# Folding the pool groups' maps and scales into the pool projection's weight, in a streaming-encoder block on one Trainium2 core

## The chip, the core and the metric

The kernel runs on one core of a Trainium2 chip. A core has five engines with queues of their own: TensorE (PE in the profile) multiplies matrices and writes PSUM, VectorE (DVE) and ScalarE (ACT) do elementwise work, GpSimd (POOL) and SyncE (SP) are used here mostly to issue transfers. Sixteen DMA engines move data between device memory and the core's SBUF. The metric is the device time of one execution in microseconds, as the median of several runs.

## What is computed

One block of a hybrid encoder on a sequence of 2048 frames with 1024 channels, in float32. The part that matters here is branch A, the pooling branch, and where its result goes:

```python
def pool_mixer(u, pool_w, pool_scale, w_pool_out):
    groups = jnp.split(u, POOL_GROUPS, axis=-1)
    pooled = jnp.stack([trailing_mean_minus_self(g, w) for g, w in zip(groups, POOL_WINDOWS)], axis=2)
    mixed = jnp.einsum('bsgc,gcd->bsgd', pooled, pool_w)
    mixed = mixed.reshape(u.shape) * pool_scale
    return mixed @ w_pool_out
...
    h = rmsnorm(x, norm_mix_pre[l])
    proj = h @ w_in[l]
...
    merged = jax.nn.sigmoid(g_a) * branch_a + jax.nn.sigmoid(g_b) * branch_b
    x = x + rmsnorm(merged @ w_o[l], norm_mix_post[l])
    h = rmsnorm(x, norm_mlp_pre[l])
    f = jnp.square(jax.nn.relu(h @ w_up[l])) @ w_down[l]
    x = x + rmsnorm(f, norm_mlp_post[l])
```

There are four pool groups of 128 channels with windows of 2, 4, 8 and 16 frames. Each group has a 128 x 128 map (`pool_w`) and a scale per channel, then all 512 channels are projected to 1024 (`w_pool_out`). Branch B is a gated convolution of 31 taps with a LayerNorm. Map, scale and projection are linear and follow each other with nothing between, so their product can be formed from the weights alone.

## The kernel before

**Numbers in two parts.** Float32 products are made of three matmuls in TensorE's fp32r format: each operand is split into a high part (ACT casts it to fp32r) and a low part (DVE subtracts the high part), and high x high, high x low and low x high are accumulated (`passes`, `matmuls`). `split` does this for data, `split_w` for weights, which live in the rings `wh` and `wl` of three tiles each; raw weights are loaded into the ring `wr` of four.

**Tiles and stages.** The sequence is cut into two batches b of 1024 tokens, and all tiles are 128 partitions by 1024. Batch 0 runs the input projection first: the GLU octets, then the pool octet, then gates a and b (`run_first`, `run`). An `Octet` is a 2 x 2 block product done in seven products by a Strassen scheme, each of 24 matmuls of 512 columns; after each it calls `flush` (which issues pending stores of kept weights) and `bg()`. Then `branch_a(0)` projects the pooled cells, and the same follows for batch 1, whose weights are partly reloaded from copies kept in device memory (`kept`). Then come `merge(0)`, the output projection of batch 0, `branch_a(1)`, the MLP of batch 0, and the rest of batch 1.

**Background lanes.** Work that is not a main product stands in generators. A `Lane` is given credit at a rate of so many steps per `bg()` call; a generator's plain `yield` ends a step, and `yield n` ends the lane's work for this call and for n - 1 further calls. The lanes carry the statistics of batch 1 (`in_stats`), the convolution (`conv_steps`, 31 taps on DVE per group at L924 and L928, four groups per batch), the pooling (`pool_steps`) and LayerNorm (`norm_steps`). `empty()` runs what is left. In batch 0 the pooling and the convolution's groups 1 to 3 form one chain at rate 3 that starts when the pool octet is done (`more`, L1562); what is left of it goes on in batch 1's lanes at rate 3.2, then 2.8.

**The pool groups.** `pool_steps` (L1012) loads a group's cell u and a window s from device memory, adds shifted windows on DVE, subtracts the cell (L1036), splits the result (L1042), multiplies it with the group's map from `pw` (L1046 to L1049, the tile `mix`), scales it by channel out of PSUM on ACT (L1051) and stores it in `mxd`. `pool_weight` (L1006) loads and splits the maps once.

**The pool projection.** `fetch` (batch 0) or `fetch_spread` (batch 1) loads the four cells of `mxd` and splits them. `branch_a` (L1089) takes four weight tiles of `w_po` with `load_w` (L234): in batch 0 a raw tile is loaded, cast and subtracted, and the low part is stored; in batch 1 the raw tile is loaded and cast, and the low part is loaded. Each weight tile serves 48 matmuls (the tile `A`); gate a is reloaded from `sad`, multiplied in (L1107), and the result goes to `mad`.

**Order.** A planner (the Tile framework's scheduler) orders each engine's instructions by priority, which is the order of tracing moved ahead by an offset: `ahead` is 260 instructions for weights. `behind` places background instructions after the main line's last one. SP's queue holds nearly all transfers and is worked in order, so that a transfer that waits for a tile holds up those behind it. Main products and fold or mix products share one ring of three PSUM tiles (`psum`).

Of the kernel before, what the change touches and what calls it, by code (L numbers as in the profile page):

```python
# [15 lines left out]
P = 128  # L16
D = 1024
# [45 lines left out]
def f32(ap):  # L63
    return ap.bitcast(F32)
# [3 lines left out]
def block_kernel(  # L68
# [35 lines left out]
    def mk(pl, tag, dt=F32, shape=(P, TB)):  # L104
        return pl.tile(list(shape), dt, tag=tag, name=nm(tag))
# [20 lines left out]
    def load(o, src):  # L126
        return nc.sync.dma_start(o, src)  # L127
# [778 lines left out]
    def conv_steps(b, groups, ahead=True):  # L906


        def get(c):
            v = window(TAPS - 1 + TB)  # L910
            load(v, vd[c][:, b * TB : b * TB + TAPS - 1 + TB])
            return v

        v = None
        for c in groups:
            if v is None:
                v = get(c)
                yield 1
            nv = None
            acc = mk(p_y, "y")  # L920
            for k in range(TAPS):
                wk = col(C_CW + c * TAPS + k)
                if k == 0:
                    nc.vector.tensor_scalar(  # L924
                        acc, v[:, :TB], wk, col(C_CB + c), op0=ALU.mult, op1=ALU.add
                    )
                else:
                    nc.vector.scalar_tensor_tensor(  # L928
                        acc, v[:, k : k + TB], wk, acc, op0=ALU.mult, op1=ALU.add
                    )  # L930
                if ahead and k == 15 and c != groups[-1]:
                    nv = get(c + 1)
                yield
            v = nv
            if c == 0:
                sums[b] = mk(p_ss, "sm")
                nc.vector.tensor_copy(sums[b], acc)
            else:
                add(sums[b], sums[b], acc)
            load(yd[b, c, 0], acc)  # L940
            yield
# [61 lines left out]

    pw = [p_const.tile([P, CW], F32R, tag=f"pw{i}", name=f"pw{i}") for i in (0, 1)]

    def pool_weight():  # L1006
        raw = mk(p_wr, "wr")[:, :CW]
        load(raw, w_pool)
        nc.scalar.copy(pw[0], raw)
        sub(pw[1], raw, f32(pw[0]))  # L1010

    def pool_steps(b, alone):  # L1012

# [8 lines left out]
        for g in range(CC):  # L1022
# [15 lines left out]
            )  # L1038
            if g + 1 == CC:
                done.add(("windows", b))  # L1040
            yield 1
            hl = split(u, *TR)  # L1042
            if g + 1 < CC:
                s, u = get(g + 1)
            yield 2
            ps = psum("mix")  # L1046
            for t in (0, 1):
                h = slice(t * T, (t + 1) * T)
                matmuls(ps[:, h], pw, g, [tuple(p[:, h] for p in hl)], main=False)  # L1049
            o = tr()  # L1050
            nc.scalar.activation(o, ps, AF.Copy, scale=col(C_PSC + g))  # L1051
            yield
            load(mxd[b, g, 0], o)
            yield

# [33 lines left out]
    def branch_a(b, mixed, bg):  # L1089
# [7 lines left out]
        keys = [(c, t) for c in range(CPS) for t in (0, 1)]  # L1097
        for (c, t), sg in ahead_by_one(keys, gate_of, 2):
            if t == 0:
                w = load_w(w_po[c], ("po", c))  # L1100
            ps = psum("A")
            for q in (0, 1):
                i = matmuls(ps[:, q * T : (q + 1) * T], w, CC * q, half(mixed, t))
# [456 lines left out]
        lanes.append(tail)  # L1560

    def more():  # L1562
        pool_weight()
        tail.gens.append(chain_of(pool_steps(0, True), conv_steps(0, (1, 2, 3), False)))
        tail.rate = 3

    pi = pool_in(0, parts)[0]
    run_first(o1, then(lambda: lanes.append(stats), then(after_glu, o2, 6)), bg, dve)
    run(
        [then(more, pi)],  # L1570
        gate(0, parts, 3, sad, "ga", "lows"),
        gate(0, parts, 5, sbd, "gb", "sums"),
        left=o2,
    )
    stats.empty()
    rest = tail.gens
    mixed = fetch(mxd, 0)
    parts = Parts(lambda ops: input_parts(1, ops))
# [12 lines left out]
    lanes += [Lane(3.2, *rest, marked(norm_steps(0, 1), "norm"))]  # L1591

    def pooling():
        lanes[0].rate = 2.8
        lanes.append(Lane(1.7, pool_steps(1, False)))
        lanes.append(Lane(1.5, behind_all(conv_steps(1, (0, 1, 2, 3)), "conv", ("windows", 1))))


# [517 lines left out]
```

## Time and profile before

| | us |
|---|---|
| median of three runs | 2207.85 |
| lowest and highest | 2205.48, 2213.11 |
| the profiled execution | 2211.62 |
| its span, from first to last instruction | 2209.8 |
| its mean granted TensorE clock | 0.991 of full speed |

The profile is of one execution. Its rows of time give the busy time of each engine, with the number of instructions behind an x; PEld is the loading of weights into TensorE, which overlaps its matmuls. A row of the timeline has the start, the duration, the engine, the line of the kernel, the operation, out<-in by the program's names, and in brackets the engine's idle time before it with what ended it. L268 is the matmul of the helper `matmuls`, L121 the subtraction helper, L118 the addition helper, L225 the cast of a weight, L127 a load or store on SP's queue. Rows of transfers end with the median time from issue to landing. PEclk is the TensorE clock that was granted, 1.00 being full speed. In a row of tiles three numbers behind a colon are the least, the median and the greatest duration in ns. Rows of groups give busy us, the mean ns of one, and the idle time before them.

In time: gates a and b of batch 0 run to 296 us, the pool projection of batch 0 to 340 us, then the pool octet and the others of batch 1; the pool projection of batch 1 runs from 758 to about 808 us, and the MLP fills the rest.

### The profile page before, as it was taken

What the parts mean: (1) busy time and instruction counts of PE and PEld (TensorE: products, weight loads), DVE (VectorE), ACT (ScalarE), POOL (GpSimd) and SP (SyncE); (2) the same over time, 40 slices, a digit from 0 to 9 for tenths busy, and PEclk for the clock granted to TensorE, in tenths of its full rate; (3) what the DMA queues carried; (4) which work ended last, traced back from release to release, by engine and by line L of the source; (5) the groups of instructions that cost most, each with busy time, mean ns of one, the idle gap of its engine ahead of it and who ended that gap; (6) DMA issues with size and microseconds to landing.
All of it is one profiled execution on the core that took longest, in us unless ns stands there. A gap on an engine that the chain in (4) does not pass through costs nothing. (4 is left out here: it accounts for less than half of the span.)

```text
span 2209.8 us, 25108 instructions
## 1 busy us (share of the span) xinstructions
PE 2167.7 (98%) x9588; PEld 1787.0 (81%) x9588; DVE 1684.4 (76%) x1637; ACT 1050.3 (48%) x1094; POOL 27.0 (1%) x51
## 2 busy tenths in 40 slices
PE   9999999999999999999999999999999999999996
PEld 7888888788888788888888878788778888888875
DVE  8997788998678898977757857776645556696667
ACT  6444454334533545555625766655444222224553
POOL 1000000000000000000000000000000000000001
PEclk9999999999999999999999999999999999999998
DMA  7688897678997687355686768976956545446798
GB/s 274 246 296 320 324 331 275 236 260 294 332 373 248 257 314 276 129 190 201 242 333 226 259 248 294 338 295 232 338 197 229 183 157 189 148 146 221 268 310 254
DMA packets 158264, 568.04 MB, mean 257 GB/s; under 512 B 17696, under 2 KB 17952, under 8 KB 158112
## 3 DMA queue, kind: packets, MB, share of 16 engines
q1 hardware_dynamic: 140608, 503.43, 64.1%
q10 hardware_dynamic: 12672, 46.14, 5.4%
q0 software_dynamic: 4864, 16.87, 2.8%
q8 instruction: 75, 1.23, 0.2%
q14 instruction: 45, 0.37, 0.0%
HBM read 378.58 MB, written 188.84 MB: 257 GB/s over the span
## 5 line engine op out<-in xcount | busy, mean ns | idle before, releaser
L268 PE MATMUL up<-big,wh 128*128 128x512 f32 x1792 | 481.0, 390 | 1.8 <-DVE big L121 1.6
L268 PEld LDWEIGHTS up<-big,wh 128*128 128x128 f32 x1792 | 336.0, 188 | 73.3 <-DVE big L121 2.7
L225 ACT CAST wh<-wr 128x1024 fp32r<-128x1024 f32 x177 | 185.7, 1051 | 313.6 <-PE up L268 72.2
L268 PE MATMUL down<-tr,wh 128*128 128x512 f32 x800 | 312.2, 390 | 0.0
L928 DVE SCALAR_TENSOR_TENSOR y<-v,cst,y 128x1024 f32<-128x1024 f32 x240 | 307.5, 1281 | 2.8
L268 PE MATMUL down<-fo,wh 128*128 128x512 f32 x784 | 303.1, 392 | 1.6 <-ACT fo L1773 1.6
L268 PE MATMUL up<-big,wl 128*128 128x512 f32 x896 | 276.5, 390 | 0.7 <-DVE wl L121 0.7
L268 PE MATMUL down<-fo,wl 128*128 128x512 f32 x768 | 238.4, 392 | 2.7 <-DMA wl<-lows 2.7
L225 ACT CAST wh<-ws 128x1024 fp32r<-128x1024 f32 x118 | 124.0, 1052 | 223.5 <-DVE ws L121 66.6
L268 PEld LDWEIGHTS up<-big,wl 128*128 128x128 f32 x896 | 168.0, 188 | 35.9 <-DVE wl L121 1.2
L118 DVE TENSOR_TENSOR big<-big,down 128x1024 f32<-128x1024 f32 x88 | 106.9, 1219 | 114.6 <-PE down L268 105.9
L1773 ACT CAST fo<-tr 128x1024 fp32r<-128x1024 f32 x86 | 86.8, 1051 | 207.9 <-PE down L268 138.3
L268 PEld LDWEIGHTS down<-tr,wh 128*128 128x128 f32 x800 | 150.7, 188 | 31.4
L268 PEld LDWEIGHTS down<-fo,wh 128*128 128x128 f32 x784 | 147.9, 189 | 33.4 <-ACT fo L1773 2.7
L268 PEld LDWEIGHTS down<-fo,wl 128*128 128x128 f32 x768 | 145.1, 189 | 33.2 <-DMA wl<-lows 3.1
L121 DVE TENSOR_TENSOR wl<-ws,wh 128x1024 fp32r<-128x1024 f32 x110 | 134.2, 1221 | 47.4 <-ACT wh L225 47.3
L121 DVE TENSOR_TENSOR wl<-wr,wh 128x1024 fp32r<-128x1024 f32 x100 | 121.9, 1220 | 31.9 <-ACT wh L225 30.3
L121 DVE TENSOR_TENSOR tr<-tr,fo 128x1024 fp32r<-128x1024 f32 x86 | 101.8, 1220 | 45.5 <-ACT fo L1773 45.5
L268 PE MATMUL wo<-big,wh 128*128 128x512 f32 x480 | 128.9, 390 | 0.0
L268 PE MATMUL glu<-big,wh 128*128 128x512 f32 x464 | 125.4, 391 | 1.2 <-ACT wh L225 0.5
L268 PE MATMUL gb<-big,wh 128*128 128x512 f32 x448 | 120.1, 390 | 0.0
L268 PE MATMUL ga<-big,wh 128*128 128x512 f32 x448 | 120.0, 389 | 0.0
(194 smaller groups left out, 3365.0 us busy)
## 6 DMA issues: line engine op xcount, KB each, us to landing
tr<-fd SPq DMA_DIRECT2D x110, 512.0 KB, 4.6
wl<-kept SPq DMA_DIRECT2D x85, 512.0 KB, 4.7
kept<-wl SPq DMA_DIRECT2D x72, 512.0 KB, 5.9
wr<-w_down SPq DMA_DIRECT2D x68, 512.0 KB, 5.4
wr<-w_up SPq DMA_DIRECT2D x64, 512.0 KB, 4.6
wr<-w_in SPq DMA_DIRECT2D x60, 512.0 KB, 5.3
fd<-tr ACTq DMA_DIRECT2D x54, 512.0 KB, 3.6
fd<-tr SPq DMA_DIRECT2D x48, 512.0 KB, 3.2
```

Source lines behind the costliest of these rows:

```text
L118: return nc.vector.tensor_tensor(o, a, b, op=ALU.add)
L121: return nc.vector.tensor_tensor(o, a, b, op=ALU.subtract)
L225: nc.scalar.copy(hi[:, :n], src[:, :n])
L268: i = nc.tensor.matmul(ps, w[wp][:, (at + k) * P : (at + k + 1) * P], rhs[k][xp], start=start and n == 0, stop=stop and n == len(order) - ...
L928: nc.vector.scalar_tensor_tensor(acc, v[:, k : k + TB], wk, acc, op0=ALU.mult, op1=ALU.add)
L1773: nc.scalar.copy(hi, t)
```

## The change

The maps and scales are now multiplied into the projection's weight once. A new generator `fold_steps` loads the maps (transposed, so that the output channel lies on the partitions), scales them by channel on ACT and splits them into `pw`. For each of the four weight tiles it loads the raw tile, splits it, multiplies it with the four maps (12 matmuls of 256 columns), splits the product, and stores both parts in device memory as `folded`. It has a lane of its own at rate 1 that starts after the second product of gate a's second octet, and is emptied before the projection of batch 0. `folded_weight` replaces `load_w` in `branch_a`: in both batches it loads both parts directly into `wh` and `wl`. `pool_steps` stores the pooled cell itself, without split, product and scaling, and yields less. The convolution's first step of a run of groups now yields 2, not 1, and two lane rates of batch 1 are 3 and 1.5 in place of 2.8 and 1.7. The columns of `w_po` lie in another order in device memory, so that a group's 256 are next to each other; the product is put back in the old order as it leaves PSUM.

```diff
@@ conv_steps
             if v is None:
                 v = get(c)
-                yield 1
+                yield 2
@@
-    def pool_weight():
-        raw = mk(p_wr, "wr")[:, :CW]
-        load(raw, w_pool)
-        nc.scalar.copy(pw[0], raw)
-        sub(pw[1], raw, f32(pw[0]))
+    folded = {(c, p): dram("folded") for c in range(4) for p in (0, 1)}
+
+    def fold_steps():
+        m = mk(p_wr, "wr")[:, :CW]
+        load(m, w_pool)
+        for g in range(CC):
+            gm = m[:, g * P : (g + 1) * P]
+            nc.scalar.activation(gm, gm, AF.Copy, scale=col(C_PSC + g))
+        nc.scalar.copy(pw[0], m)
+        sub(pw[1], m, f32(pw[0]))
+        for c in range(4):
+            raw = tr()
+            load(raw, w_po[c])
+            yield 1
+            hl = split(raw, *TR)
+            yield 2
+            ps = psum("fold")
+            for g in range(CC):
+                h = slice(g * 2 * P, (g + 1) * 2 * P)
+                matmuls(ps[:, h], pw, g, [tuple(x[:, h] for x in hl)], main=False)
+            whole = ps.rearrange("p (g q n) -> p q g n", g=CC, q=2)
+            hi, lo = tr(F32R), tr(F32R)
+            by_q = [x.rearrange("p (q g n) -> p q g n", q=2, g=CC) for x in (hi, f32(hi), lo)]
+            nc.scalar.copy(by_q[0], whole)
+            sub(by_q[2], whole, by_q[1])
+            yield 1
+            load(folded[c, 0], f32(hi))
+            load(folded[c, 1], f32(lo))
+            yield 1
+
+    def folded_weight(c):
+        with tc.high_priority(offset=ahead[0]):
+            w = mk(p_wh, "wh", F32R), mk(p_wl, "wl", F32R)
+            for p in (0, 1):
+                load(f32(w[p]), folded[c, p])
+        return w
@@ pool_steps
-            yield 1
-            hl = split(u, *TR)
+            o = u
             if g + 1 < CC:
                 s, u = get(g + 1)
             yield 2
-            ps = psum("mix")
-            for t in (0, 1):
-                h = slice(t * T, (t + 1) * T)
-                matmuls(ps[:, h], pw, g, [tuple(p[:, h] for p in hl)], main=False)
-            o = tr()
-            nc.scalar.activation(o, ps, AF.Copy, scale=col(C_PSC + g))
-            yield
             load(mxd[b, g, 0], o)
             yield
@@ branch_a
-                w = load_w(w_po[c], ("po", c))
+                w = folded_weight(c)
@@
     def more():
-        pool_weight()
...
+    fold = Lane(1.0, fold_steps())
     pi = pool_in(0, parts)[0]
+    ga = gate(0, parts, 3, sad, "ga", "lows")
+    gb = gate(0, parts, 5, sbd, "gb", "sums")
+    then(lambda: lanes.append(fold), ga[1], 2)
...
     stats.empty()
+    fold.empty()
@@ pooling
-        lanes[0].rate = 2.8
-        lanes.append(Lane(1.7, pool_steps(1, False)))
+        lanes[0].rate = 3
+        lanes.append(Lane(1.5, pool_steps(1, False)))
@@ kernel
-        "w_pool": g["pool_w"].transpose(1, 0, 2).reshape(P, CW),
-        "w_po": pairs(g["w_pool_out"]).reshape(4, P, D),
+        "w_pool": g["pool_w"].transpose(2, 0, 1).reshape(P, CW),
+        "w_po": pairs(g["w_pool_out"]).transpose(0, 1, 3, 2, 4).reshape(4, P, D),
```

More of the change, by code (lines that the diff above doesn't have):

```diff
@@ L1570, in block_kernel @@
         [then(more, pi)],
-        gate(0, parts, 3, sad, "ga", "lows"),
-        gate(0, parts, 5, sbd, "gb", "sums"),
+        ga,
+        gb,
         left=o2,
```

## The prediction

> **What bounds the kernel now.** I read the page first, for the engine that sets the pace; then the busy time by stretch, for where that engine pauses; then its waits, the timeline around the worst pause, and the transfers of the stretch that the change fills.
>
> ```profile
> span 2209.8 us, 25108 instructions
> PE 2167.7 (98%) x9588; PEld 1787.0 (81%) x9588; DVE 1684.4 (76%) x1637; ACT 1050.3 (48%) x1094; POOL 27.0 (1%) x51
> ```
>
> TensorE (PE) is busy for 98% of the span, 42.1 us short of it. A busy PE need not be at its peak, so I look at the spacing of its matmuls:
>
> ```profile
> core 0: us, PE busy (x) PEld busy (x) DVE busy (x) ACT busy (x) POOL busy (x), PEclk, DMA share, GB/s
> 186.00:345.00 159.00, 159.00 (x706) 131.59 (x705) 123.86 (x122) 80.27 (x88) 0.00 (x0) 1.00 0.93 336
> 345.00:400.00 55.00, 50.82 (x211) 40.82 (x210) 50.08 (x43) 20.20 (x20) 0.00 (x0) 0.94 0.62 214
> 396.00:400.00 4.00, 4.00 (x11) 3.11 (x10) 4.00 (x4) 1.05 (x1) 0.00 (x0) 0.50 0.52 148
> 500.00:600.00 100.00, 98.39 (x442) 81.38 (x441) 75.72 (x78) 51.10 (x52) 0.00 (x0) 1.00 0.87 316
> 750.00:815.00 65.00, 62.60 (x276) 51.23 (x275) 60.78 (x64) 30.11 (x37) 4.84 (x9) 0.97 0.84 315
> 1610.00:2085.00 475.00, 475.00 (x2100) 393.37 (x2098) 303.22 (x262) 170.15 (x174) 0.00 (x0) 1.00 0.56 186
> ```
>
> From 1610 to 2085 us 2100 matmuls take 475 us, 226 ns each, at a granted clock of 1.00: there a 512-column matmul costs 226 ns of end time. From 186 to 345 us, where the weight is to be folded, PE has no idle time either. So the kernel is bound by its count of matmuls, plus a few pauses. Two pauses lie where the change reaches: 345 to 400 us (55.00 - 50.82 = 4.2 us) and 750 to 815 us (2.4 us). Each also lowers the granted clock: (1 - 0.94) x 55 = 3.3 us more in the first, (1 - 0.97) x 65 = 2.0 us in the second. The 1.6 us that PE lacks from 500 to 600 us left the clock at 1.00. The first pause in detail, from PE's waits in that stretch and the timeline:
>
> ```profile
> PE pool L268 <- DVE tr L118: 2.7, 1, 2.7
> PE pool L268 <- DVE big L121: 1.5, 1, 1.5
> ...
> 352.14 7.89 DVE L928 SCALAR_TENSOR_TENSOR y<-v,cst,y 128x1024 f32<-128x1024 f32 x6
> 363.36 1.23 DVE L118 TENSOR_TENSOR ws<-wr,wr 128x1024 f32<-128x1024 f32 x1 [3.34 <-DMA wr<-w_in]
> 390.31 1.22 DVE L118 TENSOR_TENSOR tr<-pool,tr 128x1024 f32<-128x1024 f32 x1
> 391.67 1.39 PE L268 MATMUL pool<-big,wh 128*128 128x512 f32 x5 [2.67 <-DVE tr L118]
> ...
> L928 DVE SCALAR_TENSOR_TENSOR y<-v,cst,y 128x1024 f32<-128x1024 f32 x240 | 307.5, 1281 | 2.8
> ```
>
> At 363 us DVE had been idle; after that its rows follow each other without a gap until the block sum of 390.31 us, which holds a PSUM tile of the pool projection, comes too late. What fills DVE there is the depthwise convolution's taps (L928, 1.28 us each), mixed with the token operands.
>
> **What it removes.** Per batch and group, a product of the pooled cell with the group's map: two halves of three matmuls (L1047 to L1049), 8 x 6 = 48 in all, between the octets' matmuls:
>
> ```profile
> 219.48 0.39 PE L268 MATMUL gb<-big,wl 128*128 128x512 f32 x1
> 219.71 1.56 PE L268 MATMUL mix<-tr,pw 128*128 128x512 f32 x6
> 221.10 1.55 PE L268 MATMUL gb<-big,wh 128*128 128x512 f32 x6
> ...
> L1051 ACT ACTIVATE tr<-mix,cst x8: 1095/1109/1122, 197.9 to 546.3; 128x1024 f32<-128x1024 f32 x8
> L218 ACT CAST tr<-tr 128x1024 fp32r<-128x1024 f32 x8 | 8.4, 1046 | 1.8 <-DVE tr L1036 1.8
> L121 DVE TENSOR_TENSOR tr<-tr,tr 128x1024 fp32r<-128x1024 f32 x8 | 9.7, 1218 | 0.0
> L121 DVE TENSOR_TENSOR wl<-wr,wh 128x1024 fp32r<-128x1024 f32 x100 | 121.9, 1220 | 31.9 <-ACT wh L225 30.3
> ```
>
> The six start at 219.71 and the next product at 221.10: 1.39 us. PE has no gap there, so all of it is on the path: 8 x 1.39 = 11.1 us. Beside PE go eight casts and eight scaled copies on ACT (8 x 1.05 + 8 x 1.11 = 17.3 us), eight subtractions on DVE (9.7 us) and, in the projection, eight casts and, in batch 0, four subtractions of the projection's raw weight (8.4 us ACT, 4.9 us DVE). ACT and DVE work under PE, so I count these at nothing by themselves.
>
> **What it adds on PE.** Folding multiplies four weight tiles by four maps, three matmuls each: 48 matmuls again, of 256 columns. The trace has none of that width; its neighbours are one column and 128:
>
> ```profile
> 151.60 0.95 PE L554 MATMUL rb<-inv_d,tr 128*128 128x1 f32 x8
> 152.40 1.65 PE L268 MATMUL ga<-big,wh 128*128 128x512 f32 x6
> ...
> 735.58 0.27 PE L644 MATMUL rb<-ident,sp 128*128 128x128 f32 x1
> 735.69 0.27 PE L644 MATMUL rb<-ident,sq 128*128 128x128 f32 x1
> ```
>
> One column costs (152.40 - 151.60) / 8 = 100 ns, 128 columns 110 ns, 512 columns 226 ns. So 256 columns lie between 110 (a weight load still sets the pace) and 226 ns (no saving by width); half of 226 is 113 and the straight line between 128 and 512 gives 149. I take 125, nearest to the half: 48 x 0.125 = 6.0 us, with 5.3 and 10.8 us as the ends. The Trainium skill, "TensorE: Matmul & The Clock Gate", section "Back-to-back issue gap", gives 262 cycles for 256 columns, some 109 ns at 2.4 GHz, an estimate of 5.2 us; for 512 it gives 518 cycles, 216 ns, where the row here has 226, and by it PE would save 0.8 us more. By the rows PE saves 11.1 - 6.0 = 5.1 us, between 0.3 and 5.8.
>
> **What it adds elsewhere.** On DVE four splits of the raw weight and four subtractions out of PSUM, by the 1.22 us row 9.8 us (twice that for the four from PSUM if their regrouped order is slow); on ACT eight copies and four short scalings, about 9 us. In the 159 us from 186 to 345 us DVE is busy 123.9, so 35 us of idle time hide the 9.8; without that cover each microsecond would delay a weight's low half. A fold product holds one of three PSUM tiles until DVE has subtracted, a mix product only until ACT had read it. An octet needs two at once, so I take nothing, with one late subtraction of 1.2 us as the other end.
>
> Twelve more transfers of 512 KB (four raw tiles, eight stores) go through SP's queue while the second gates run; the projections move as many as before (hi and low in place of raw and low, or in place of raw and a store of the low). The new wait is at the head of each pool projection: both halves now land directly in the wh and wl rings of three, so their issue must wait for the third product back. What is behind such a load on SP's queue is everything else: gate reloads, stores of kept lows, the next raw weights. From the transfers and SP's waits (240 to 296 us, and 296 to 345 us for the gate reloads):
>
> ```profile
> SPq L127 <- DVE wl L121: 20.1, 6, 4.6
> wr<-w_po SPq DMA_DIRECT2D x4, 512.0 KB, 5.6
> tr<-sad SPq DMA_DIRECT2D x8, 512.0 KB, 8.3
> ...
> L127 SPq DMA_DIRECT2D wr<-w_po x4: 332/333/447, 265.1 to 285.4; - x4
> ```
>
> The slot comes free two products of 24 matmuls (24 x 0.226 = 5.4 us), so 10.9 us, before the projection. Two issues of 0.33 us, a landing of 5.6 to 8.3 us and SP's own hold of 0 to 4.6 us make 6.3 to 13.6 us. The middle, 9.9, fits; I take no wait, with 2.7 us at each of the two projections as the other end.
>
> **What it moves.** The pool's generator loses its split and product, so in batch 0 it ends about four background calls earlier (I count 18 calls at three steps each before, 14 after), and the convolution's group 1 starts earlier: some nine to twelve taps of 1.28 us move from behind 345 us to before it. Its group boundary then falls ahead of 390 us, not on it, and the new pause of two calls there leaves out one call of 3.2 taps: 3.7 us less for DVE between 363 and 390 us. The pause of 4.2 us is thus shortened by 0 (if other work fills the room) to 3.7 us. I take half, 1.9. What is left, 2.3 us, is like the pause at 750 to 815 us, which cost 2.0 us of clock, against 3.3 now: 1.3 more, say 1.7 with the shorter span at half clock. Gain 3.6 us, ends 0 and 7. The lane rates of batch 1 (3 for 2.8, 1.5 for 1.7) change DVE's load by 0.2 taps a product, 0.26 us of 5.4, in a stretch where PE does not wait for DVE; nothing.
>
> **Sum.** -11.1 + 6.0 - 3.6 = -8.7 us. The profiled execution took 2211.6 us (its span 2209.8 and 1.8 around it), 3.8 above the median of 2207.85, so it would become 2202.9 and the median 2199.2. I forecast 2199.
>
> **The rivals.** (1) PE's saving alone: the pause at 390 us stays, because the planner puts other taps in the room. For it speaks that the lane's rate is unchanged; against it, that DVE's backlog there is a sum with little slack. 2207.85 - 5.1 = 2202.7.
>
> (2) Both pauses go: freed casts on ACT and subtractions on DVE around the second projection also remove the one at 750 to 815 us. -5.1 - 4.2 - 3.3 - 2.4 - 2.0 = -17.0: 2190.9. Against it: that pause comes from the pooled cells' own splits, which stay.
>
> (3) Slower: transfers can't keep up between 186 and 345 us.
>
> ```profile
> DMA packets 4785, 17.49 MB, mean 324 GB/s; under 512 B 528, under 2 KB 528, under 8 KB 4782
> DMA packets 5107, 18.68 MB, mean 334 GB/s; under 512 B 558, under 2 KB 558, under 8 KB 5103
> DMA packets 4751, 17.30 MB, mean 353 GB/s; under 512 B 534, under 2 KB 534, under 8 KB 4749
> ...
> GB/s 408 428 395 415 405 324 247 385 408 428 415 221 311 314 301 361 375 288 415 421 415 415 114 214 405 211 211 338 421 425 421 418 418 405 415 415 385 395 184 237
> ```
>
> These are 186 to 240, 240 to 296 and 296 to 345 us: 53.5 MB in 159 us at 0.90 to 0.96 busy. With 12 x 0.524 = 6.3 MB more it is 59.8 MB, 376 GB/s. If 353, the best of the three, is all there is, it takes 169.4 us, 10.4 us late, and a wait like that halves the clock for 3.3 us more: -5.1 + 10.4 + 3.3 = +8.6, 2216.5. It decides once the ceiling is under 59.8 / (159 + 5.1) = 364 GB/s. Against it: stores and the next batch's inputs can slip without harm, and in the last row, 40 slices from 296 to 345 us, half of them stand over 400 GB/s. The Trainium skill, "DMA: Bandwidth & Descriptors", section "Bandwidth", holds that transfers between HBM and SBUF are bound at about 358 GB/s per core; by it the stretch would take 167 us, 8.0 us late, an estimate of 2214. The 353 row does not contradict it over 49 us; the slices do for a microsecond or two.
>
> (4) It does not do what it says: a 256-column matmul costs nearly what a 512-column one does, PE saves 0.3 us, and no pause changes: 2207.5. Against it: the 110 ns row.
>
> **Chances.** What a measurement of this kernel can tell from no change is about 0.3%, 6.6 us. The forecast (2195 to 2201) has 0.38, rival 2 0.12; both are faster by more than that: 0.50. Rival 1 has 0.27 and rival 4 with partial losses 0.06, within 0.3%: 0.33. Rival 3 has 0.17, slower. The range from 2190 to 2211 leaves out the upper part of rival 3 (0.14) and a little below rival 2 (0.05).
>
> **What would show it.** Right: no mix product; 48 fold matmuls of 256 columns at 110 to 150 ns; the wait for the block sum near 390 us under 2.5 us; PE without a wait for wh or wl at the head of either projection; a mean transfer rate over 370 GB/s from 186 to 345 us. Wrong: a PE wait on DMA for wh or wl there, with the granted clock at 0.50 after it; a fold spacing near 226 ns; transfers stuck at some 350 GB/s with later weights late; DVE full from 240 us on, so that low halves come after PE needs them; or new pauses elsewhere, since the planner orders all queues anew.

## The result and the profile after

The changed kernel takes **2216.1 us** (median of 19 runs, 2210.69 to 2222.15) against 2208.03 us of the kernel before beside it (19 runs). The ratio is 1.003 with a 95% interval of 1.0021 to 1.004: 8 us slower, where 9 us faster was forecast. Its profiled execution took 2216.87 us, with a span of 2215.1.

First the head of the page and the busy time by stretch, for the stretches of the prediction.

```profile
span 2215.1 us, 25072 instructions
PE 2164.9 (98%) x9588; PEld 1787.4 (81%) x9588; DVE 1681.8 (76%) x1633; ACT 1035.1 (47%) x1082; POOL 27.0 (1%) x51
```

```profile
186.00:345.00 159.00, 147.13 (x665) 121.67 (x664) 125.61 (x129) 71.90 (x82) 0.00 (x0) 0.98 0.96 360
240.00:296.00 56.00, 45.95 (x209) 37.73 (x208) 40.16 (x47) 24.06 (x25) 0.00 (x0) 0.94 0.90 328
296.00:345.00 49.00, 49.00 (x223) 40.78 (x222) 41.02 (x35) 20.40 (x27) 0.00 (x0) 1.00 1.01 394
345.00:400.00 55.00, 55.00 (x244) 45.56 (x243) 47.87 (x41) 24.70 (x25) 0.00 (x0) 1.00 0.76 256
500.00:600.00 100.00, 97.26 (x428) 79.74 (x426) 79.62 (x81) 51.42 (x52) 0.00 (x0) 0.98 0.89 311
750.00:815.00 65.00, 63.01 (x285) 51.70 (x284) 59.50 (x62) 29.28 (x37) 6.45 (x12) 1.00 0.87 328
1610.00:2085.00 475.00, 475.00 (x2088) 393.42 (x2089) 300.75 (x259) 168.82 (x172) 0.00 (x0) 1.00 0.56 187
```

The columns are those of the prediction's table: PE, PEld, DVE, ACT and POOL busy, granted clock, DMA share, GB/s. The stretch from 186 to 345 us, where TensorE was busy throughout before, now has 11.9 us of idle time. The clock of 0.94 from 240 to 296 us stands for some 6.8 us at half clock, from 289.5 to 296.3 us. Two rows with PE's columns alone (PE busy, granted clock, DMA share, GB/s) split it:

```profile
289.60:292.32 2.72, 0.00 (x0) 0.50 0.97 354
292.32:296.20 3.88, 3.88 (x9) 0.50 0.90 306
```

In the first 2.8 of the 6.8 us PE stood still anyway, so the half clock costs it half of the other 4.0 us, 2.0 us. The stretch from 345 to 400 us, which lacked 4.2 us at a clock of 0.94, is now full at 1.00. So the stretch that was to hide the fold lost time, and the one behind it gained more than was forecast.

The first projection matmul of batch 0 dates this. From the rows of tile `A`, before and then after:

```profile
L268 PE MATMUL A<-big,wh x128: 389/389/389, 296.1 to 339.1; 128*128 128x512 f32 x128
```

```profile
L268 PE MATMUL A<-big,wh x128: 388/389/397, 312.5 to 355.6; 128*128 128x512 f32 x128
```

The projection begins 16.4 us later: 1.5 us of it is already there at the first matmul of gate a, 11.9 are new pauses, 2.0 were lost to the half clock; the fold's matmuls (5.7 us) and the four removed mix products of batch 0 (5.6 us) cancel, and the last 1.0 us was not followed up. The projection itself takes 43.1 us in both. The span grows by only 5.3 us, so everything behind that point is 11.1 us shorter. PE's waits from 180 to 315 us name the pauses (us in total, times, longest):

```profile
PE gb L268 <- ACT tr L430: 5.6, 1, 5.6
PE gb L268 <- DVE wl L121: 2.3, 1, 2.3
PE gb L268 <- ACT wh L225: 2.1, 1, 2.1
PE ga L268 <- ACT tr L430: 1.8, 1, 1.8
```

The largest is a wait for a **held copy** (L430): ACT copies a partial product of gate b out of PSUM, and the product that stops needs that tile. The timeline of ACT around it, and of PE (start, duration; in brackets the idle time before and its releaser):

```profile
280.71 1.05 ACT L1088 CAST big<-big 128x1024 fp32r<-128x1024 f32 x1
282.11 1.06 ACT L1088 CAST big<-big 128x1024 fp32r<-128x1024 f32 x1 [0.35 <-DMA big<-mxd]
284.81 1.05 ACT L1088 CAST big<-big 128x1024 fp32r<-128x1024 f32 x1 [1.64 <-DMA big<-mxd]
287.51 1.05 ACT L225 CAST wh<-ws 128x1024 fp32r<-128x1024 f32 x1 [1.65 <-DVE s L124]
288.46 1.04 ACT L225 CAST wh<-wr 128x1024 fp32r<-128x1024 f32 x1
289.41 1.04 ACT L1088 CAST big<-big 128x1024 fp32r<-128x1024 f32 x1
290.35 1.00 ACT L1031 CAST tr<-fold 128x1024 fp32r<-128x1024 f32 x1
291.26 1.93 ACT L430 COPY tr<-gb 128x1024 f32<-128x1024 f32 x2
```

```profile
292.32 2.07 PE L268 MATMUL gb<-big,wh 128*128 128x512 f32 x4 [5.60 <-ACT tr L430]
```

PE stops at 292.32 - 5.60 = 286.72 us. Both held copies stand in ACT's queue behind the casts of the four pooled cells (L1088), two weight casts (L225) and the fold's copy (L1031). From 286.72 us ACT first waits until 287.51, then does four of these until 291.26, then the copy. In the kernel before, the same place of ACT's queue reads so:

```profile
280.42 1.01 ACT L430 COPY tr<-gb 128x1024 f32<-128x1024 f32 x1
281.33 2.96 ACT L1063 CAST big<-big 128x1024 fp32r<-128x1024 f32 x3
286.23 1.05 ACT L1063 CAST big<-big 128x1024 fp32r<-128x1024 f32 x1 [1.95 <-DMA big<-mxd]
```

There the held copy goes first and the cells' casts (L1063 in that file) after it; that one of them waits 1.95 us for its transfer harms nobody.

### The profile page after: what moved, and what is told of

It reads as the page before. It is cut to its first block, busy times and chain, and to the rows that moved or that the text cites. A ratio compares the mean times of both kernels' runs of the same rounds, so it can differ in the third digit from the quotient of the medians.

```text
span 2215.1 us, 25072 instructions
## 1 busy us (share of the span) xinstructions
PE 2164.9 (98%) x9588; PEld 1787.4 (81%) x9588; DVE 1681.8 (76%) x1633; ACT 1035.1 (47%) x1082; POOL 27.0 (1%) x51
## 5 line engine op out<-in xcount | busy, mean ns | idle before, releaser
L225 ACT CAST wh<-wr 128x1024 fp32r<-128x1024 f32 x169 | 177.6, 1052 | 308.5 <-PE up L268 74.9
L268 PE MATMUL down<-tr,wh 128*128 128x512 f32 x800 | 312.5, 391 | 0.0
L225 ACT CAST wh<-ws 128x1024 fp32r<-128x1024 f32 x118 | 124.0, 1052 | 225.3 <-DVE ws L121 78.8
L121 DVE TENSOR_TENSOR wl<-wr,wh 128x1024 fp32r<-128x1024 f32 x96 | 116.9, 1219 | 25.2 <-ACT wh L225 23.4
```

The costliest lines, as they stand in the source:

```text
L121: return nc.vector.tensor_tensor(o, a, b, op=ALU.subtract)
L225: nc.scalar.copy(hi[:, :n], src[:, :n])
L268: i = nc.tensor.matmul(ps, w[wp][:, (at + k) * P : (at + k + 1) * P], rhs[k][xp], start=start and n == 0, stop=stop and n == len(order) - ...
```

## The experiments

Fifteen kernels were run, 4 to 12 times each, beside the kernel before (whose medians were 2208.8 to 2209.1 us). The table gives for each the median, the ratio's interval, the first projection matmul of batch 0 by its trace, and the largest pause of PE between gate a's start and the end of that projection with what ended it.

| run | median us | 95% interval | projection from, us | largest pause before its end |
|---|---|---|---|---|
| before (profile) | 2208 | | 296.1 | none |
| after | 2216.1 | 1.0021–1.0040 | 312.5 | 5.60, held copy |
| no_fold | 2212.3 | 1.0003–1.0032 | 310.1 | 10.44, held copy |
| traffic_only | 2218.7 | 1.0022–1.0048 | 312.1 | 5.59 weight cast, 5.55 held copy |
| compute_only | 2214.2 | 1.0005–1.0034 | 310.1 | 7.45, held copy |
| pool_queue | 2224.8 | 1.0043–1.0084 | 319.9 | 11.77, held copy |
| before_new_pace | 2220.7 | 1.0027–1.0060 | 310.8 | 7.18, held copy |
| before_pool_pace | 2222.2 | 1.0043–1.0076 | 307.1 | 5.89, held copy |
| before_b1_pace | 2211.5 | 0.9995–1.0031 | 296.3 | none |
| pin_cells | 2216.0 | 1.0015–1.0046 | 314.3 | 3.81, held copy |
| pin_all | 2213.1 | 1.0004–1.0039 | 311.6 | 2.81, weight's low part |
| old_pace | 2213.1 | 1.0002–1.0030 | 301.5 | 5.97, product of `A` |
| mixed_pace | 2222.5 | 1.0043–1.0085 | 299.4 | 3.71, product of `A` |
| two_yields | 2248.0 | 1.0151–1.0193 | 300.7 | 4.84, product of `A` |
| two_yields_aside | 2242.3 | 1.0129–1.0167 | 301.2 | 6.11, product of `A` |
| mixed_early | 2233.7 | 1.0095–1.0147 | 320.9 | 14.99, weight cast |
| old_aside | **2205.0** | **0.9969–0.9990** | 302.5 | 2.95, weight cast |

**Is it the fold?** The first four runs took the fold apart: no fold at all; its transfers without its work; its work without its stores; its transfers on GpSimd's queue. The first three leave out what branch A needs: where nothing is folded or stored, the projection loads kept low parts of gate a's weights instead, and traffic_only stores the raw weight.

```diff
# no_fold
-    fold = Lane(1.0, fold_steps())
...
# no_fold and compute_only
-                load(f32(w[p]), folded[c, p])
+                load(f32(w[p]), kept[("ga", 3 + p), 1 + c, "low"])
# traffic_only
-            hl = split(raw, *TR)
...
-            load(folded[c, 0], f32(hi))
-            load(folded[c, 1], f32(lo))
+            load(folded[c, 0], raw)
+            load(folded[c, 1], raw)
# compute_only
-            load(folded[c, 0], f32(hi))
-            load(folded[c, 1], f32(lo))
# pool_queue
-            load(raw, w_po[c])
+            aside(raw, w_po[c])
...
-            load(folded[c, 0], f32(hi))
-            load(folded[c, 1], f32(lo))
+            aside(folded[c, 0], f32(hi))
+            aside(folded[c, 1], f32(lo))
```

> The changed kernel without the fold lane: nothing is folded or stored, and both projections load kept low parts of gate a's weights in place of the folded weight (so the result of branch A is not the reference's). Everything else of the change stays: no product per pooled cell, direct loads into wh and wl, the new lane rates. If the fold costs what the changed kernel lost (both theories), the projection of batch 0 starts 15 to 18 us before the changed kernel's 312.4 us, near 290 to 296, PE's waits from 180 us to there are under 2 us in place of 11.9, and the time is 13 to 18 us under the changed kernel's 2216, near 2200. If moved taps and rates are the cause, the waits stay and the time is only some 6 us lower, by the 48 matmuls.

> The fold lane keeps its twelve transfers of 512 KB at the same places (four raw tiles in, eight stores of the raw tile out) and leaves out the split, the 48 matmuls and the copies out of PSUM; the stored weight is the raw one, so branch A is not the reference's. Theory 1, the transfers are the cause (engines full, SP's queue held): most of the 11.9 us of PE waits before the projection stay, 8 or more, the transfer rate from 186 to 312 us is near 350 GB/s, and the time is 2207 to 2212 (the 5.7 us of fold matmuls gone). Theory 2, the fold's work on ACT and DVE and its PSUM and tr tiles, which stand in the queues before the octets' own, is the cause: the waits fall under 4 us and the time is near 2200.

> The fold lane keeps its four raw loads, splits, matmuls and copies, but stores nothing; the projections load kept low parts of gate a's weights, so branch A is not the reference's. Theory 1 (transfers): with 8 of the 12 transfers gone the waits fall to 4 us or less, and the time is some 2204 to 2207 (5.7 us of fold matmuls above the kernel without a fold). Theory 2 (work and tiles on the engines): the waits stay at 8 us or more and the time is 2211 to 2216.

> The changed kernel with the fold's twelve transfers issued on POOL's queue in place of SP's; the bytes and the result are the same. Theory 1 in its form 'the DMA engines are full': no change, 2212 to 2218, waits near 11.9 us. Theory 1 in its form 'SP's queue is held by stores that wait for DVE': the waits fall under 5 us and the time is 2204 to 2209. Theory 2: no change either.

Without the fold, without its 48 matmuls and its twelve transfers, the kernel is still slower than before (2212.3 us), and the same wait is there, larger. PE's waits of that run from 180 to 315 us:

```profile
PE gb L268 <- ACT tr L430: 10.4, 1, 10.4
PE ga L268 <- ACT tr L430: 1.8, 1, 1.8
```

In all four the last pause before the projection ends on a held copy, of 5.55 to 11.77 us, whatever part of the fold is gone. So neither its transfers nor its work is the cause of that wait, though without the fold the time is some 4 us lower than with it. The times of traffic_only and pool_queue lie above all that was expected of them, and in traffic_only a pause of 5.59 us on a weight cast has come in ahead of the held copy's; why these two are slower than the changed kernel was not followed up. What all four share with the changed kernel is the pacing of the background work: the pool steps have two yields less, the convolution's first yield is longer, and batch 1's lane rates are 3 and 1.5 in place of 2.8 and 1.7. That became theory 3: with the new pacing the pooled cells are stored earlier, and the planner puts what depends on them ahead of the held copies in ACT's queue. The last store of a pooled cell of batch 0, before and then after:

```profile
275.17 0.32 SPq L127 DMA_DIRECT2D mxd<-tr  x1
```

```profile
253.04 0.48 SPq L127 DMA_DIRECT2D mxd<-tr  x1
```

**The pacing alone.** The direct test leaves the algebra of the kernel before as it is (mix matmuls, no fold) and takes over only the pacing; a second run takes over only the two missing yields; a third only the pacing of batch 1.

```diff
# before_new_pace, at the start of a convolution's group
-                yield 1
+                yield 2
# before_new_pace and before_pool_pace, in the pool steps
-            yield 1
             hl = split(u, *TR)
...
-            yield
             load(mxd[b, g, 0], o)
# before_new_pace and before_b1_pace, for batch 1
-        lanes[0].rate = 2.8
-        lanes.append(Lane(1.7, pool_steps(1, False)))
+        lanes[0].rate = 3
+        lanes.append(Lane(1.5, pool_steps(1, False)))
# before_b1_pace, in the pool steps, for both yields
-            yield 1
+            if b == 0:
+                yield 1
```

> The kernel before, with its mix matmuls kept and no fold, but with the new pacing of the pool steps, the convolution steps and the lane rates. Theory 3: the wrong order of ScalarE's queue comes with the pacing alone, a pause of 5 to 11 us before the first projection matmul and 3.4 to 6.8 us of half clock, so 2214 to 2222, slower than before though no fold and no added transfer is in it. Rival 1: no added transfer, so 2205 to 2211, as before.

> The kernel before, with its mix matmuls, but without the two yields in the pool steps; rates and convolution as before. Theory 3: the same wrong order, a pause of 5 us or more at 285 to 300 us with 3.4 us or more of half clock, 2214 to 2222, as in the run of the kernel before with all of the new pacing. Rival 6: no pause there, 2205 to 2211.

> The kernel before with its mix matmuls, and the new pacing for batch 1 alone (pool steps without the two yields, rates 3 and 1.5). Theory 3: batch 0 runs as before, without a pause up to the first projection matmul at 294 to 299 us; the pauses of 2.67 and 1.50 us at 391 to 395 us go, and 2 to 3.4 us of half clock behind them: 2201 to 2206. Rival 5: the pauses stay and the time is 2207 to 2211.

The new pacing alone makes the kernel before 11.6 us slower (2220.67), and the two yields alone 13.2 us (2222.22). The wait and the queue are there again. PE's wait of before_new_pace from 270 to 315 us, and its ACT timeline:

```profile
PE gb L268 <- ACT tr L430: 7.2, 1, 7.2
```

```profile
275.34 1.04 ACT L1061 CAST big<-big 128x1024 fp32r<-128x1024 f32 x1
...
282.97 1.05 ACT L1061 CAST big<-big 128x1024 fp32r<-128x1024 f32 x1 [4.69 <-DMA big<-mxd]
285.66 1.04 ACT L225 CAST wh<-ws 128x1024 fp32r<-128x1024 f32 x1 [1.65 <-DVE sy L601]
286.62 1.04 ACT L225 CAST wh<-wr 128x1024 fp32r<-128x1024 f32 x1
287.56 2.56 ACT L724 ACTIVATE big<-big,cst 128x512 f32<-128x512 f32 x4
290.02 1.89 ACT L430 COPY tr<-gb 128x1024 f32<-128x1024 f32 x2
```

The cells' casts (L1061), one of which waits 4.69 us for its transfer, two weight casts and even four operations on the next batch's input (L724) stand ahead of the two held copies. Nothing of the fold is in this kernel. The pacing of batch 1 alone brings no such pause and, against the expectation of 2201 to 2206, no gain: 2211.54 us, an interval that holds 1, and the pauses of 2.53 and 1.51 us near 391 us stay.

**The order put back by hand.** Two runs of the changed kernel force the order in ACT's queue: the cells' casts behind the last held copy (pin_cells), and also each weight's casts behind the held copies of three products earlier (pin_all).

```diff
+            helds.append(i.ins)
...
+    at = len(nc.cur_bb.bb.instructions)
     mixed = fetch(mxd, 0)
+    after_held(at)
# pin_all
+            old = [h for n, h in held_at if n <= njob[0] - 3]
+            for k in nc.cur_bb.bb.instructions[at:]:
+                if old and k.engine == mybir.EngineType.Activation:
+                    tc.add_manual_dep(k, old[-1].name, NOSYNC, reason="after the held copy")
```

> The changed kernel, with the casts of batch 0's pooled cells put behind the last held copy of gate b in ScalarE's queue; the casts of the octet weights still stand ahead of the held copies. Theory 3: only a part of the pause at 292 us goes, since the octet weight's casts still wait for VectorE and the store: 2 to 4 us of pause are left, the time is 2207 to 2214. Rival 1: 2214 to 2218, as the traffic is the same. Rival 4 (the casts of the pooled cells come late then, and the projection waits for them): a new pause of over 3 us at the first projection matmul, 2216 or more.

> As the run before it, and the casts of each octet weight also stand behind the held copies of three jobs earlier, so that both held copies of gate b's end go first, then the octet's casts, then the cells'. Theory 3: no pause over 2.5 us at 285 to 300 us, the first projection matmul at 300 to 306 us, the time 2198 to 2209. Rival 1: 2214 to 2218. Rival 4 (casts of cells now late): a pause at the first projection matmul, 2212 or more.

The first leaves 3.81 us of the wait for the held copy at 293 us, since the weight casts still stand ahead of it, and gains nothing (2216.0). In the second PE waits for no held copy any more between 180 and 315 us; its two largest waits there are these:

```profile
PE gb L275 <- DVE wl L121: 3.7, 2, 2.8
PE gb L275 <- ACT wh L232: 3.6, 2, 2.0
```

But it waits for weights instead: these casts, now held back, come late for later products. The projection begins at 311.6 us, not at the 300 to 306 expected, and the time is 2213.05 (expected 2198 to 2209). With the order changed the wait for the held copy is gone, but swapping the order by force only moves the pause.

**The old pacing with the fold.** The third way is to keep the change and go back to the pacing of the kernel before: throughout (old_pace), for batch 0's pool steps and both batches' convolution (mixed_pace), by the two yields alone (two_yields), and as mixed_pace with the fold one octet earlier (mixed_early).

```diff
# old_pace, against the changed kernel; two_yields has the two pool lines only
-                yield 2
+                yield 1
...
             o = u
+            yield 1
...
             yield 2
+            yield
             load(mxd[b, g, 0], o)
...
-        lanes[0].rate = 3
-        lanes.append(Lane(1.5, pool_steps(1, False)))
+        lanes[0].rate = 2.8
+        lanes.append(Lane(1.7, pool_steps(1, False)))
# mixed_early, beside the pacing
-    then(lambda: lanes.append(fold), ga[1], 2)
+    then(lambda: lanes.append(fold), ga[0], 2)
```

> The changed kernel with the pacing of the kernel before (the yields of the pool steps and of the convolution steps, and the lane rates 2.8 and 1.7); fold, transfers and folded weight stay. Theory 3 (the new pacing lets the pooled cells be cast ahead of the held copies of gate b in ScalarE's queue, and TensorE waits for those): the held copies stand ahead of the casts of the pooled cells again, the 5.60 us pause at 292 us and the half clock behind it (3.4 us) go, the first projection matmul comes at 300 to 305 us instead of 312.5, the time is 2198 to 2208, below the changed kernel by 8 or more. Rival 1 (the fold's 12 transfers and their bandwidth are the cause): they are all still there, the time stays at 2214 to 2218.

> The changed kernel with the pacing of the kernel before for batch 0 (yields of its pool steps, and the convolution steps) and the new pacing for batch 1 (pool steps without the two yields, rates 3 and 1.5). Theory 3 (each pace is good or bad by the order it gives ScalarE's and VectorE's queues at one place): no pause at 285 to 300 us, as in the run with the old pacing throughout; the pause at 340 us (5.97 us, a product that stands in VectorE's queue behind the next batch's input, which ScalarE waits for) stays; the pauses at 400 to 410 us (1.99 and 1.50 us) go. So 3 to 5 below the run with the old pacing throughout: 2207 to 2211. Rival 5 (the pace has nothing to do with the pause at 390 to 410; it went in the changed kernel because the projection came later there): the pauses of 1.99 and 1.50 us stay, 2212 to 2215.

> The changed kernel with the two yields that the change took out of the pool steps put back, and nothing else. Theory 3 (those two yields alone decide whether the pooled cells' casts come ahead of the held copies): no pause over 2.5 us at 285 to 300 us, the first projection matmul at 299 to 303 us instead of 312.5; a pause of 3 to 6 us at 337 to 341 us as in the runs with the old pacing, since the folded weight's loads still stand ahead of the next batch's input: 2207 to 2214. Rival 6 (the convolution's yield or the rates make the order): the pause of 5.6 us at 292 us stays, 2214 to 2218.

> As mixed_pace, and the fold begins one octet earlier (behind the third job of gate a's first octet instead of its second). Theory 3: the fold's last transfers and loads are out of the queue before the next batch's input is asked for, so that this input lands before 320 us and ScalarE no longer waits 23 us for it; the pause at 340 us goes with the half clock behind it (3.4 us), and no pause over 2.5 us is left from 110 to 410 us: 2195 to 2203, below the kernel before. Rival 1 (the fold's 12 transfers of 6.3 MB cost the time, wherever they are put): pauses of gate a and gate b in their place, 2209 to 2216.

In old_pace, mixed_pace and two_yields the pause at 292 us is gone as theory 3 has it, and the projection begins at 299.4 to 301.5 us, 11 to 13 us sooner than in the changed kernel. The times are not what was expected, all the same. In old_pace (2213.06, expected 2198 to 2208) a new pause stands inside the projection. Its waits from 325 to 345 us:

```profile
ACT big L724 <- DMA big<-xt: 23.2, 1, 23.2
DVE big L124 <- ACT big L724: 7.4, 2, 6.4
...
PE A L268 <- DVE tr L124: 6.0, 1, 6.0
```

Read from the bottom: PE waits 6.0 us for a PSUM tile until DVE has multiplied gate a into it; DVE's product stands behind work on the next batch's input; that waits for ACT (L724), and ACT waited 23.2 us for the transfer of that input. Its transfers were late in being issued. SP's timeline of the same run:

```profile
309.59 0.32 SPq L127 DMA_DIRECT2D wl<-folded  x1
...
312.94 0.60 SPq L127 DMA_DIRECT2D wh<-folded  x1
...
316.54 0.32 SPq L127 DMA_DIRECT2D wl<-folded  x1
...
318.05 6.90 SPq L127 DMA_DIRECT2D big<-xt  x8
```

All eight input transfers are issued from 318.05 us on, behind the folded weight's loads, which wait and hold the queue meanwhile: between 285 and 320 us SP waits 10.2 us for stores of low parts out of `wl`, 9.6 us for products of gate b, and 3.0 us for a store of the fold itself to land. In the kernel before, the first four input transfers were issued between 286 and 294 us.

The other three runs missed by more. In mixed_early the pause of 14.99 us comes at 136 us: a product of the pool octet waits for a weight cast there, so this earlier fold is worse. In two_yields 16.9 us of pauses lie between the projection and tile `B`'s first matmul (5.9 in the kernel before), and 8.4 more up to 1156 us. It differs from old_pace by the convolution's yield and the lane rates alone, and is 35 us slower; which of them does it was not tried by itself. mixed_pace keeps pauses of 1.82 and 0.84 us near 402 us, and its median is 2222.48, some 5 us over its profiled execution.

**The folded loads on another queue.** The last theory (7) says that the pause at 340 us comes from SP's queue. The test changes one line of old_pace, and of two_yields:

```diff
-                load(f32(w[p]), folded[c, p])
+                aside(f32(w[p]), folded[c, p])
```

> The changed kernel with the pacing of the kernel before throughout, and the folded weight's eight loads issued from GpSimd's queue instead of SyncE's. Theory 7 (the pause at 340 us comes from SyncE's queue: the loads of the folded weight wait there for a weight buffer, and the next batch's input, its ScalarE work and VectorE's products stand behind them): the input is issued before 312 us instead of 318, ScalarE's wait of 23.2 us shrinks below 12, and the pause of 5.97 us at 340 us with its half clock goes: 2200 to 2207, and A's stage is 43.5 us as before. Rival 1 (the bandwidth of the added transfers, wherever they are issued): the pause stays over 3 us, 2211 to 2215. Rival 8 (loads from GpSimd's queue come late): a wait for them at the first or a later projection product of over 3 us, 2212 or more.

> Both: the two yields put back, and the folded weight's loads on GpSimd's queue. Theory 3 with theory 7: no pause over 2.5 us from 110 to 345 us, 2198 to 2206, below the kernel before. Rival 1: 2211 to 2217. Rival 8: a wait of over 3 us at a projection product, 2210 or more.

With the eight loads on GpSimd's queue, **old_aside takes 2205.01 us, and is faster than both kernels** (interval against before 0.9969 to 0.999). The waits of PE from 108 to 412 us, and the issue of the input, from the rows of tile `big`:

```profile
PE gb L268 <- ACT wh L225: 2.9, 1, 2.9
PE pool L268 <- DVE tr L118: 1.8, 1, 1.8
PE pool L268 <- DVE big L121: 1.5, 1, 1.5
```

```profile
L127 SPq DMA_DIRECT2D big<-xt x8: 327/492/1806, 288.2 to 319.8; - x8
...
  DMA big<-xt: 15.6, 3
```

The input's issue begins at 288.2 instead of 318.1 us, ACT's longest wait for it falls from 23.2 to 11.5 us, no product of `A` waits any more, and the projection takes 43.1 us again. The same twelve added transfers are in it, so bandwidth was not the cause of that pause. GpSimd now does the waiting, and from 280 to 340 us nothing but these eight loads is in its queue:

```profile
290.09 0.54 POOL L131 DMA_DIRECT2D wh<-folded  x1 [259.93 <-PE gb L268]
...
314.77 0.54 POOL L131 DMA_DIRECT2D wh<-folded  x1 [12.10 <-DMA folded<-tr]
```

In two_yields_aside the line gains 5.7 us, but at 2242.29 it is far from the 2198 to 2206 expected: a pause of 6.11 us on the projection's product stays, and DVE waits 5.8 us for the fold's copy on ACT (L1031) there. The pauses behind the projection stay as well. One control is missing: no run gave the kernel before another queue for its projection's loads. PE waits for nothing in it between 108 and 345 us, so there is no pause that this could remove there, but it was not measured.

## Why the prediction was wrong, point by point

**The pace of PE** held: 475 us for 2088 matmuls from 1610 to 2085 us, 12 records fewer than before, and a few can be missing from a trace. **What it removes** held too: no mix product is left. **What it adds on PE** was sized right. From the timeline of the changed kernel:

```profile
274.23 1.58 PE L268 MATMUL fold<-tr,pw 128*128 128x256 f32 x12
275.65 0.86 PE L268 MATMUL gb<-big,wh 128*128 128x512 f32 x3
```

Twelve fold matmuls in 1.42 us are 118 ns each, 5.7 us for 48 where 6.0 were predicted. The Trainium skill, "TensorE: Matmul & The Clock Gate", section "Back-to-back issue gap", gives 262 cycles for 256 columns as the gap of a matmul taken by itself, some 109 ns as an estimate; the trace is 9 ns above it, as its 226 was 10 above the 216 by the same table for 512 columns. So PE's own saving is 11.1 - 5.7 = 5.4 us.

**What it adds elsewhere** was put at nothing. At the head of the projection that held: the projection took 43.1 us with no wait. The sentence that "what is behind such a load on SP's queue is everything else" was right, but it priced only the projection; in old_pace it was the next batch's input behind those loads that cost a pause of 5.97 us, and 2.0 us more by the half clock (337.5 to 344.3 us, PE back at 340.3). In the changed kernel itself that did not come to the surface, since the input's transfers were issued from 296.5 us on.

**What it moves is the step that failed.** The prediction saw that the pool's generator ends about four background calls earlier, and counted that as gain only: taps moved into free time on DVE, -3.6 us. It did not ask what else then becomes ready earlier: the last pooled cell is stored 22 us sooner, and the planner placed the casts of the reloaded cells, and in before_new_pace even the next batch's input, ahead of held copies that PE needs at once. This is worth +11.6 us with all of the pacing and +13.2 us with the two yields alone, measured in the kernel before without any fold. The prediction wrote that ACT and DVE work lies under PE and costs nothing "by themselves"; that is true of the work and not of its place in a queue. ACT was busy for only 47% of the span, and for 43% of the stretch from 240 to 296 us with the pause in it (24.06 of 56 us).

**The pause near 390 us** went away whole: 4.2 us of pause, and of clock 2.9 us rather than the 3.3 that the prediction read (half clock from 393.7 to 400.5 us, with PE back only at 394.57), where 3.6 in all were forecast. The taps moved as forecast: from 240 to 345 us DVE does 20 of them (12 before), from 345 to 400 us 14 (22 before). That alone is not enough: before_pool_pace does 26 and 16 and keeps a pause of 5.61 us. In before_new_pace, which adds the convolution's longer yield and the rates, the pause is away (67.00 us of 67.00 busy from 345 to 412 us, clock 1.00); its split and its mix products are still there, so the removed work is not needed for it. With batch 1's pacing alone 2.53 and 1.51 us stay, and in old_aside, which lacks the split but has the old pacing, 1.78 and 1.50. This fits the forecast's reason, earlier taps and a longer yield, but no run changed that yield by itself, and in both kernels without the pause the stretch also comes some 15 us later. Which of these removes it stays open, and that the gain came out larger than forecast may be luck.

**The lane rates** "nothing": not settled. Together with the convolution's yield they make 35 us of difference between two_yields and old_pace, and the two were not separated. In the kernel before, the rates with batch 1's pool yields made no difference that can be told from none (before_b1_pace).

**Rival 3** gave 2216.5, close to the 2216.1 measured, by luck: its mechanism is wrong. It needed a ceiling of transfers under 364 GB/s. The changed kernel moved 360 GB/s over 159 us while PE stood still for 11.9 of them, and 394 over the 49 us from 296 us, with PE fully busy. The Trainium skill, "DMA: Bandwidth & Descriptors", section "Bandwidth", has about 358 GB/s per core for transfers between HBM and SBUF, as each core's share when both cores of a pair stream. This kernel runs on one core, and its rate of 394 is above 358, so as a ceiling for this stretch it does not hold. The prediction's own row of slices already spoke against a ceiling near 360, and for longer than "a microsecond or two": eight slices in a row, 9.8 us, stand at 405 GB/s or more. And without the added transfers the pause is larger (no_fold). That the planner orders all queues anew stood among the signs of a wrong forecast, but with no price and no chance.

The **sum** by what was measured, for the profiled executions: PE's matmuls -5.4, the pause near 390 us and its clock -7.1, new pauses before the projection +11.9 and what the half clock took +2.0, the later first matmul of gate a +1.5: +2.9. From 500 to 600 us there are 1.1 us more of pause and 1.7 of clock, and from 750 to 815 us 0.4 and 1.7 less: +3.6 in all, against +5.3 measured (2216.87 - 2211.6). The remaining 1.7 us was not followed up.

With the old pacing and the loads on GpSimd's queue (old_aside) the change is worth -4.0 us on the medians. Beside it stand 5.4 us of PE's own work saved and some 6 us lost before the projection, to one pause of 2.95 us and 3.0 us by its half clock, partly won back by smaller pauses behind it. With the loads on SP's queue (old_pace) it is +4.0 us. So the saving on PE is real, but how much of the -4.0 the algebra would bring by itself is not shown.

## What to carry to other kernels

When a change shortens background work, list what then becomes ready earlier on **each in-order queue**, and look for the short instruction behind it that the bounding engine waits for: an engine at 47% cost 5.6 to 11.8 us here by what stood ahead of a 1 us copy. Hold the pacing constant when testing an algebraic change, and test the pacing alone in the old kernel; here the pacing alone cost 11.6 us, and the algebra with the old pacing gained 4.0 us once its loads had left SP's queue. A load into a tile that comes free late belongs on a queue with nothing urgent behind it.

## What the runs showed of the hardware

A pause's price in clock is not fixed. In the changed kernel pauses of 1.82, 2.12 and 2.33 us left the granted clock at 1.00, while in two_yields the same pause of 1.82 us at 188 us and in old_pace one of 1.62 us at 247 us were followed by a stretch of 3.4 us at half clock, and in old_aside one of 2.95 us runs into a stretch of 6.8 us. Such a stretch costs half of the time that PE works in it: 3.0 us in old_aside, where it begins 0.9 us before PE is back, and 2.0 in the changed kernel, where it begins 2.8 us before. The loads issued from GpSimd's queue took longer to land than from SP's (9.7 and 12.1 us for `wh` and `wl` from 285 to 330 us, against 6.8 and 5.6 in old_pace), which the early issue covered. Whether the queue is the reason is not shown: transfers on SP's queue landed later too (gate a's reload 11.7 against 9.1 us), while 406 GB/s were moved against 351. And the transfers went on rising with demand: from 300 to 345 us old_aside moved 408 GB/s at a DMA share of 1.02 while PE was busy without a gap.

```profile
300.00:345.00 45.00, 45.00 (x206) 1.00 1.02 408
```

The columns here are PE busy, granted clock, DMA share and GB/s.
